# Hybrid encoder block: gate products added into the merged rows by transfers, in the last branch's seven-product scheme

## The chip, the cores and the metric

One core of one Trainium2 chip. The core has a matrix engine (PE; its weight loads are listed apart as PEld), a vector engine (DVE), a scalar engine (ACT), GpSimd (POOL) and SyncE (SP), each with its own in-order queue of instructions, and 16 DMA engines that move the transfers which SP, ACT and POOL issue. The metric is device microseconds of one execution, as the median of several runs.

## The reference

One layer of an encoder, applied to 256 + 512 = 768 tokens of width 1024 in float32. Three token mixers (a state-space branch, a differential attention, a cross-attention) give `branches`, which are projected, gated, merged and projected again:

```python
br = jnp.einsum('blnc,ncd->blnd', branches, w_branch[li])
gates = jax.nn.sigmoid((gl + b_gate[li]).astype(F32)).reshape(Bsz, L, N_BRANCH, D_MODEL)
merged = jnp.sum(gates * br.astype(F32), axis=2).astype(x.dtype)
x = x + merged @ w_out[li]
```

A SwiGLU feed-forward block with its own norm and residual follows. The kernel computes a sigmoid as (1 + tanh(x/2)) / 2 and puts the factor 1/2 where merged is split (below).

## The kernel before, in words

**Precision.** Every float32 operand of a large product is split into a high and a low float32r part, and a product is three matmuls per block of 128 (`mm3`, L755 to L757): high x high, high x low, low x high. The high part is an ACT copy, the low part a DVE subtraction of the high part from the source.

**Stages.** Norm and projections, state-space scan, differential attention, cross-attention; then the branch projections (w_branch2 and w_branch0 as plain products in `branch`, w_branch1 in `branch7`), w_out (`out_rows`), the feed-forward blocks and the down projection. The change is in `branch7` and in the weight stream's `_split_w` for it.

**branch7** (L1648 to L1700) multiplies w_branch1 (1024 x 1024) with the 1024 x 768 output of the differential attention by a seven-product scheme of the Strassen-Winograd kind. It works in four chunks of 256 output columns; in each, seven products of a 128-wide output block with 384 tokens, each product summing four blocks of 128 (twelve matmuls). The left factors are the weight blocks A11, A12, A22 and sums S1 to S4 of them, made per chunk; the right factors B11, B21, B22, T1 to T4 are made once, before (L1616 to L1653; T4 lies in the last two rows of MG). One PSUM bank, `chain`, accumulates A11·B11, then also S2·T2, then also S3·T3, and is copied out after each step by ACT; a second, `p5`, takes S1·T1 and later also S4·B22. Two SBUF accumulators, `cs[0]` = (c11, c12) and `cs[1]` = (c21, c22), collect the four output quarters with ACT copies (L1683, L1685, L1687, L1690) and DVE adds from PSUM (`plus`, L1673). They come from the pool `stg`, two buffers with the tag "brr".

**Gates and merge.** For each chunk two rows of gate logits are loaded from DRAM by POOL's queue into tiles `gs[0]`, `gs[1]` (pool `gtp`, two buffers, tag "glr"; L1657), and ACT takes their tanh in place (L1658). `merge(m)` then multiplies (1 + gate) with the accumulator on DVE, in place in `cs[m]` (L1677), adds the product to row 2c + m of `merged` (L1678: on POOL for m = 0, on DVE for m = 1), and splits that row, times 1/2, into MG's high part (ACT, L1679) and low part (DVE, L1680). MG is the left factor of w_out's product. In chunks 0 to 2 the product S4·B22 and merge(0) come ahead of A22·T4 and merge(1); in chunk 3 the other way round, since the last split overwrites T4's place in MG.

**The weight stream.** `WStream` loads weight blocks (SP's queue, L539, three raw buffers), and `_split_w` makes the seven left factors of a block. For w_branch1 (kind "w2", `inplace`) the sums use two buffers: s1 and s2 take one each, s3 takes s1's, and s4 overwrites s2 (POOL, L574, L575, L581, L583). `_factor` splits each left factor into a half of a pair of tiles, high on ACT (L557) and low on DVE (L558); four such pairs rotate (whi and wlo, `bufs=4`), so eight halves are there for the seven factors of a chunk, and a pair is written again when both of its halves have been used. A name such as wl_A in the profile is that of the pair's first factor: wl_A holds a pair that began with an A block, wl_S one that began with a sum. Other weights go through `_split` (ACT L599; DVE L605, or an accumulating transfer from POOL, L603).

**Order.** The kernel is written with a framework that tracks dependences and puts each engine's instructions in order by itself, from a simulation of their times (the context at L2031 is opened with `schedule_with_timeline_sim=True`); the source order is a priority, not the order of execution, except where an instruction is pinned to it. So PE may work on a product of the next chunk while one of this chunk waits for its factor. The order is fixed when the kernel is built.

**Behind it.** `out_rows` (L1720) multiplies rows 0 to 3 of MG (kh = 0) and then rows 4 to 7 (kh = 1) with w_out for six tiles of tokens, and adds the sum to the input x, loaded by POOL (L1707) into the place of T2 and T3.

Of the kernel before, what the change touches and what calls it, by code (L numbers as in the profile page):

```python
# [8 lines left out]
F32 = mybir.dt.float32  # L9
F32R = mybir.dt.float32r  # L10
I32 = mybir.dt.int32
AF = mybir.ActivationFunctionType
# [491 lines left out]
class WStream:  # L504
# [56 lines left out]
    def _split_w(self, i, h, inplace=False):  # L561
        gt = self.nc.gpsimd.tensor_tensor
        add, sub = ALU.add, ALU.subtract
        view = lambda t: t.rearrange("p (k m c) -> p m k c", k=4, m=2)
        new = lambda k: self.sums.tile([128, 4, 128], F32, name=f"ws{i}{k}", tag="ws")
        if h == 0:
            return
        a1, a2 = view(self.raw.pop(2 * i)), view(self.raw.pop(2 * i + 1))
        A11, A21, A12, A22 = a1[:, 0], a1[:, 1], a2[:, 0], a2[:, 1]
        self._factor(i, "A11", A11)  # L570
        s1, s2 = new(0), new(1)
        if not inplace:
            s3, s4 = new(2), new(3)
        gt(out=s1, in0=A21, in1=A22, op=add)  # L574
        gt(out=s2, in0=s1, in1=A11, op=sub)  # L575
        self._factor(i, "A12", A12)
        self._factor(i, "S2", s2)
        self._factor(i, "S1", s1)
        if inplace:
            s3, s4 = new(2), s2  # L580
        gt(out=s3, in0=A11, in1=A21, op=sub)  # L581
        self._factor(i, "S3", s3)
        gt(out=s4, in0=A12, in1=s2, op=sub)  # L583
        self._factor(i, "S4", s4)
        self._factor(i, "A22", A22)

    def _split(self):
        i, h = divmod(self.n_split, 2)
# [42 lines left out]
def hybrid_block(ctx, tc, A, outs, consts):  # L631
    nc = tc.nc
    v, act, gp, pe = nc.vector, nc.scalar, nc.gpsimd, nc.tensor
    mul, add, sub = ALU.mult, ALU.add, ALU.subtract
# [17 lines left out]
    def uid(s):  # L652
        cnt[0] += 1
        return f"{s}_{cnt[0]}"
# [88 lines left out]
    def split_evac(hi, lo, src, scale=None):  # L743

        if scale is None:
            act.activation(hi, src, AF.Copy)
            v.tensor_tensor(out=lo, in0=src, in1=hi.bitcast(F32), op=sub)
        else:
            act.activation(hi, src, AF.Copy, scale=scale)
            v.scalar_tensor_tensor(out=lo, in0=src, scalar=scale, in1=hi.bitcast(F32), op0=mul, op1=sub)  # L750

    def mm3(ps, wh, wl, xh, xl, start, stop, more=False):

        kw = {"skip_group_check": True} if more else {}
        pe.matmul(ps, wh, xh, start=start, stop=False, **kw)  # L755
        pe.matmul(ps, wh, xl, start=False, stop=False, **kw)  # L756
        pe.matmul(ps, wl, xh, start=False, stop=stop, **kw)  # L757
# [67 lines left out]
    def rows_pair(nm, off=16):  # L825
        t = hp_.tile([128, 16 * TOK + 16], F32R, name=nm, tag="X")
        return tuple(t[:, o : o + 8 * TOK].rearrange("p (k t) -> p k t", k=8) for o in (off, off + 8 * TOK))
# [152 lines left out]
    with tc.tile_pool(name="nrm", bufs=1) as pool, tc.tile_pool(name="nrmg", bufs=1) as pg:  # L980
# [35 lines left out]
        for t in range(4):  # L1016

            tc.keep_in_program_order(v.scalar_tensor_tensor(out=xm[t], in0=xm[t], scalar=1.0, in1=xm[t], op0=mul,
                                                            op1=mul, accum_out=mss[:, t : t + 1]))
# [91 lines left out]
    with ExitStack() as c2:  # L1111
# [4 lines left out]
        for c in range(12):  # L1116
            W.by_dma = True
            w = W.get()
            for m in range(2):
                M = 2 * c + m  # L1120
                for sg, (c0, n) in enumerate(SEGS):
# [3 lines left out]
                    out = act.activation(gt[:, 0:n], ps[:, 0:n], AF.Identity, bias=bg[:, M : M + 1])  # L1125
# [372 lines left out]
    with ExitStack() as c5:  # L1498
# [5 lines left out]
        merged = mgp.tile([128, 8, TOK], F32, name="merged")  # L1504
# [86 lines left out]
        for c in range(4):  # L1591
# [8 lines left out]
            for m in range(2):  # L1600
                M = 2 * c + m
# [43 lines left out]
        MG = rows_pair("mgd", 0)  # L1645
        RB["T4"] = tuple(t[:, 6:8].rearrange("p a (b t) -> p (a b) t", b=2) for t in MG)

        def branch7(n_):  # L1648
            for c in range(4):
                w = W.get()  # L1650
                if c == 0:
                    for k in range(4):
                        split_evac(RB["T4"][0][:, k], RB["T4"][1][:, k], t4[:, k])  # L1653
                gs = []
                for m in range(2):
                    g = gtp.tile([128, TOK], F32, name=uid("glr"), tag="glr")
                    gp.dma_start(g, gl_scr[8 * n_ + 2 * c + m])  # L1657
                    act.activation(g, g, AF.Tanh, scale=0.5)  # L1658
                    gs.append(g)
                cs = [stg.tile([128, TOK], F32, name=uid("bs"), tag="brr") for _ in range(2)]  # L1660
                (c11, c12), (c21, c22) = ((t[:, h1], t[:, h2]) for t in cs)
                chain = env.psb("brc")[:, 0:HT]

                def prod(l, r, ps=None, start=True):
                    if ps is None:
                        ps = psd("br")[:, 0:HT]
                    (wh, wl), (xh, xl) = w[l], RB[r]
                    for k in range(4):
                        mm3(ps, wh[:, k], wl[:, k], xh[:, k], xl[:, k], start and k == 0, k == 3, not start)
                    return ps  # L1670

                def plus(o, ps):
                    v.tensor_tensor(out=o, in0=o, in1=ps, op=add)  # L1673

                def merge(m):
                    M = 2 * c + m
                    v.scalar_tensor_tensor(out=cs[m], in0=gs[m], scalar=1.0, in1=cs[m], op0=add, op1=mul)  # L1677
                    (v if m else gp).tensor_tensor(out=merged[:, M], in0=merged[:, M], in1=cs[m], op=add)  # L1678
                    act.activation(MG[0][:, M], merged[:, M], AF.Copy, scale=0.5)  # L1679
                    v.scalar_tensor_tensor(out=MG[1][:, M], in0=merged[:, M], scalar=0.5,  # L1680
                                           in1=MG[0][:, M].bitcast(F32), op0=mul, op1=sub)

                act.activation(c11, prod("A11", "B11", chain), AF.Copy)  # L1683
                plus(c11, prod("A12", "B21"))
                act.activation(c12, prod("S2", "T2", chain, False), AF.Copy)  # L1685
                p5 = prod("S1", "T1")
                act.activation(c22, p5, AF.Copy)  # L1687
                prod("S3", "T3", chain, False)
                plus(c22, chain)
                act.activation(c21, chain, AF.Copy)  # L1690
                if c < 3:
                    plus(c12, prod("S4", "B22", p5, False))
                    merge(0)
                    plus(c21, prod("A22", "T4"))
                    merge(1)
                else:
                    plus(c21, prod("A22", "T4"))
                    merge(1)
                    plus(c12, prod("S4", "B22", p5, False))
                    merge(0)  # L1700

        branch7(1)
        fctx.close()
        x1t = xp.tile([128, TILES, 1024], F32, name="x1", tag="x1")
# [247 lines left out]
    with ExitStack() as c7:  # L1952
# [12 lines left out]
        for i, (p, g) in enumerate(ITEMS):  # L1965
# [10 lines left out]
            for t in range(3):  # L1976
                c = slice(128 * t, 128 * t + 128)
# [3 lines left out]
            if g == NG - 1:  # L1981
                r, f, op = HOME[p]
# [53 lines left out]
```

## Time and profile before

| | |
|---|---|
| median of 3 runs | 1742.41 us (1741.29 to 1743.65) |
| the profiled execution | 1743.06 us |
| its span, first to last instruction | 1741.3 us |
| mean granted PE clock | 0.999 |
| instructions | 29531 |
| DMA moved | 234.09 MB, mean 134 GB/s |
| branch7, first product to first product of w_out | 1120.74 to 1183.75 us |

How to read it: the profile is one execution on the chip; times are microseconds from the span's start unless marked ns. Matmuls overlap in the pipeline, so a matmul's duration is longer than the step from one start to the next, and a busy PE is judged by the steps. In a row of the order of time stand start, duration, engine, line, operation, output <- inputs and shape; in brackets the engine's idle time just before and what ended it. In the view of waits stand the engine and line that waited, what it waited for, the total in us, how often, and the longest. Times on POOL are rough.

### The profile page before, as it was taken

The numbers are of one execution on the slowest core, as the hardware profiler recorded it, in microseconds if no ns is written. First come the engines' busy times: TensorE is split into PE (matmuls) and PEld (weight loads), VectorE is DVE, ScalarE is ACT, GpSimd is POOL, SyncE is SP. The second block draws the span as 40 slices with busy tenths as digits, with TensorE's granted clock in tenths as the row PEclk, the third lists the DMA queues.
The fourth block names the chain that finished last, engine by engine and source line by source line (L and its number), as shares of the span: only waits on it lengthen the run. The fifth ranks groups of instructions, "written<-read, shape, count | busy, mean of one in ns | idle before, by whom it ended". The sixth has DMA issues, their size and how long they took to land.

```text
span 1741.3 us, 29531 instructions
## 1 busy us (share of the span) xinstructions
PE 1726.6 (99%) x11188; PEld 1608.1 (92%) x11188; DVE 1300.5 (75%) x2405; ACT 908.6 (52%) x1924; POOL 302.5 (17%) x308
## 2 busy tenths in 40 slices
PE   9999999999999999999999999999999999999999
PEld 9999988999999999999989888998889999998887
DVE  7665749699999778887886536685598777776775
ACT  7444543776767346877765434353343333334443
POOL 0000000000000100111000001341036555541130
PEclk9999999999999999999999999999999999999999
DMA  7222636755556454745653435335312323239974
GB/s 268 78 85 91 125 120 135 186 125 143 145 159 159 115 140 103 164 91 156 155 165 117 140 116 157 103 111 174 97 55 91 110 91 109 92 110 295 248 157 97
DMA packets 209213, 234.09 MB, mean 134 GB/s; under 512 B 57832, under 2 KB 173296, under 8 KB 209072
## 3 DMA queue, kind: packets, MB, share of 16 engines
q1 hardware_dynamic: 182160, 167.49, 32.0%
q0 software_dynamic: 17440, 58.34, 15.6%
q10 hardware_dynamic: 9472, 6.39, 1.3%
q8 instruction: 88, 1.44, 0.4%
q14 instruction: 53, 0.43, 0.1%
HBM read 165.78 MB, written 41.22 MB: 119 GB/s over the span
## 4 chain that ended last, share of the span: by engine, by line
PE 95%; DVE 2%; ACT 1%; issue 0%; DMA 0%; POOL 0%; SPq 0%; ACTq 0%; DVEq 0%
PE gl L755 4%; PE gl L756 4%; PE gl L757 4%; PE gate L755 3%; PE gate L756 3%; PE up L756 3%; PE gate L757 3%; PE up L755 3%; PE up L757 3%; PE dn L757 3%; PE dn L755 3%; PE dn L756 3%; PE br L755 3%; PE br L757 3%; PE br L756 3%; PE qk L755 3%
## 5 line engine op out<-in xcount | busy, mean ns | idle before, releaser
L599 ACT ACTIVATE wh<-wr 128x1024 fp32r<-128x1024 f32 x116 | 131.9, 1138 | 52.3 <-PE br L756 13.3
L605 DVE TENSOR_TENSOR wl<-wr,wh 128x1024 fp32r<-128x1024 f32 x74 | 99.2, 1342 | 63.5 <-ACT wh L599 61.7
L755 PE MATMUL gl<-H,wh 128*128 128x256 f32 (+1 forms) x384 | 132.2, 344 | 0.0
L757 PE MATMUL gl<-H,wl 128*128 128x256 f32 (+1 forms) x384 | 129.0, 336 | 0.0
L756 PE MATMUL gl<-H,wh 128*128 128x256 f32 (+1 forms) x384 | 128.7, 335 | 0.0
L603 POOL DMA_DIRECT2D wl<-wr x42 | 36.6, 872 | 483.3 <-ACT wl L602 464.1
L755 PE MATMUL qk<-wh,H 128*128 128x256 f32 x384 | 108.3, 282 | 0.0
L756 PE MATMUL qk<-wl,H 128*128 128x256 f32 x384 | 108.0, 281 | 0.0
L757 PE MATMUL qk<-wh,H 128*128 128x256 f32 x384 | 107.3, 279 | 0.0
L558 DVE TENSOR_TENSOR wl_S<-ws,wh_S 128x512 fp32r<-128x512 f32 x84 | 70.7, 863 | 26.2 <-ACT wh_S L557 26.2
L756 PE MATMUL dn<-wld,dxh 128*128 128x512 f32 x231 | 89.6, 389 | 0.0
L755 PE MATMUL dn<-whd,dxh 128*128 128x512 f32 x231 | 89.5, 389 | 0.0
L757 PE MATMUL dn<-whd,dxl 128*128 128x512 f32 x231 | 88.9, 389 | 0.0
L557 ACT ACTIVATE wh_S<-ws 128x512 fp32r<-128x512 f32 x84 | 49.5, 625 | 73.5 <-PE up L756 36.6
L757 PEld LDWEIGHTS gl<-H,wl 128*128 128x128 f32 x384 | 72.0, 188 | 8.1
L756 PEld LDWEIGHTS gl<-H,wh 128*128 128x128 f32 x384 | 72.2, 188 | 7.2
L755 PEld LDWEIGHTS gl<-H,wh 128*128 128x128 f32 x384 | 72.3, 188 | 6.9
L757 PEld LDWEIGHTS qk<-wh,H 128*128 128x128 f32 x384 | 72.6, 189 | 0.6
L755 PEld LDWEIGHTS qk<-wh,H 128*128 128x128 f32 x384 | 72.4, 188 | 0.6
L756 PEld LDWEIGHTS qk<-wl,H 128*128 128x128 f32 x384 | 72.3, 188 | 0.5
L1296 DVE TENSOR_REDUCE nm<-sc 128x1 f32<-128x512 f32 (+1 forms) x96 | 56.7, 597 | 18.1 <-PE sc L1291 17.2
L1298 ACT ACTIVATE p<-sc,nm 128x512 f32<-128x512 f32 (+1 forms) x96 | 58.8, 615 | 14.4 <-DVE nm L1296 13.9
(535 smaller groups left out, 6076.2 us busy)
## 6 DMA issues: line engine op xcount, KB each, us to landing
wr<-in_w_in_dram SPq DMA_DIRECT2D x48, 512.0 KB, 5.0
wr<-in_w_gate_up_dram SPq DMA_DIRECT2D x44, 512.0 KB, 3.6
wl<-wr POOLq DMA_DIRECT2D x42, 512.0 KB, 5.4
wr<-in_w_branch_dram SPq DMA_DIRECT2D x24, 512.0 KB, 4.5
glr<-gl_scr POOLq DMA_DIRECT2D x24, 384.0 KB, 3.5
hid_scr<-fa SPq DMA_DIRECT2D x11, 768.0 KB, 6.4
wr<-in_w_mem_kv_dram SPq DMA_DIRECT2D x16, 512.0 KB, 4.4
wr<-in_w_in_dram SPq DMA_DIRECT2D x32, 256.0 KB, 3.9
```

The lines of the kernel that those rows point to most:

```text
L557: self.nc.scalar.activation(f(hi), src, AF.Copy)
L558: self.nc.vector.tensor_tensor(out=f(lo), in0=src, in1=f(hi).bitcast(F32), op=ALU.subtract)
L599: self.nc.scalar.activation(hi, r, AF.Copy)
L603: self.nc.gpsimd.dma_start(lo, r.bitcast(F32R), accum_op=ALU.add)
L605: self.sub.tensor_tensor(out=lo, in0=r, in1=hi.bitcast(F32), op=ALU.subtract)
L755: pe.matmul(ps, wh, xh, start=start, stop=False, **kw)
L756: pe.matmul(ps, wh, xl, start=False, stop=False, **kw)
L757: pe.matmul(ps, wl, xh, start=False, stop=stop, **kw)
L1296: v.tensor_reduce(out=nm[:, m : m + 1], in_=ps, axis=AX.X, op=ALU.max, negate=True)
L1298: act.activation(pm[:, 0:n], ps, AF.Exp, bias=nm[:, m : m + 1], accum_out=s1s[:, tt : tt + 1] if m == 0 else s2)
```

## The change

In `branch7`, for chunks 0 to 2, `merge` writes the product of gate and accumulator into the gate's tile and adds it to the row of `merged` by an accumulating transfer that POOL issues; the split of the two rows into MG is emitted in the next chunk, behind the copy of c21. In chunk 3 the add is on DVE for both rows, and the split follows at once. The two accumulator tiles change roles in odd chunks. S1's product is emitted ahead of S2's, with the copy of p5 ahead of the copy of c12, and A22·T4 with merge(1) ahead of S4·B22 with merge(0) in all chunks. In `_split_w` the factor of A22 is made ahead of that of S4 for this kind of block alone; blocks of the feed-forward part keep their order.

```diff
--- before.py
+++ after.py
@@ -581,8 +581,8 @@
         gt(out=s3, in0=A11, in1=A21, op=sub)
         self._factor(i, "S3", s3)
         gt(out=s4, in0=A12, in1=s2, op=sub)
-        self._factor(i, "S4", s4)
-        self._factor(i, "A22", A22)
+        for key, src in (("A22", A22), ("S4", s4)) if inplace else (("S4", s4), ("A22", A22)):
+            self._factor(i, key, src)
 
     def _split(self):
         i, h = divmod(self.n_split, 2)
@@ -1645,6 +1645,11 @@
         MG = rows_pair("mgd", 0)
         RB["T4"] = tuple(t[:, 6:8].rearrange("p a (b t) -> p (a b) t", b=2) for t in MG)
 
+        def merged_parts(M):
+            act.activation(MG[0][:, M], merged[:, M], AF.Copy, scale=0.5)
+            v.scalar_tensor_tensor(out=MG[1][:, M], in0=merged[:, M], scalar=0.5,
+                                   in1=MG[0][:, M].bitcast(F32), op0=mul, op1=sub)
+
         def branch7(n_):
             for c in range(4):
                 w = W.get()
@@ -1658,6 +1663,8 @@
                     act.activation(g, g, AF.Tanh, scale=0.5)
                     gs.append(g)
                 cs = [stg.tile([128, TOK], F32, name=uid("bs"), tag="brr") for _ in range(2)]
+                if c % 2:
+                    cs.reverse()
                 (c11, c12), (c21, c22) = ((t[:, h1], t[:, h2]) for t in cs)
                 chain = env.psb("brc")[:, 0:HT]
 
@@ -1674,30 +1681,28 @@
 
                 def merge(m):
                     M = 2 * c + m
-                    v.scalar_tensor_tensor(out=cs[m], in0=gs[m], scalar=1.0, in1=cs[m], op0=add, op1=mul)
-                    (v if m else gp).tensor_tensor(out=merged[:, M], in0=merged[:, M], in1=cs[m], op=add)
-                    act.activation(MG[0][:, M], merged[:, M], AF.Copy, scale=0.5)
-                    v.scalar_tensor_tensor(out=MG[1][:, M], in0=merged[:, M], scalar=0.5,
-                                           in1=MG[0][:, M].bitcast(F32), op0=mul, op1=sub)
+                    v.scalar_tensor_tensor(out=gs[m], in0=gs[m], scalar=1.0, in1=cs[m], op0=add, op1=mul)
+                    if c < 3:
+                        gp.dma_start(merged[:, M], gs[m], accum_op=add)
+                    else:
+                        v.tensor_tensor(out=merged[:, M], in0=merged[:, M], in1=gs[m], op=add)
+                        merged_parts(M)
 
                 act.activation(c11, prod("A11", "B11", chain), AF.Copy)
                 plus(c11, prod("A12", "B21"))
-                act.activation(c12, prod("S2", "T2", chain, False), AF.Copy)
                 p5 = prod("S1", "T1")
                 act.activation(c22, p5, AF.Copy)
+                act.activation(c12, prod("S2", "T2", chain, False), AF.Copy)
                 prod("S3", "T3", chain, False)
                 plus(c22, chain)
                 act.activation(c21, chain, AF.Copy)
-                if c < 3:
-                    plus(c12, prod("S4", "B22", p5, False))
-                    merge(0)
-                    plus(c21, prod("A22", "T4"))
-                    merge(1)
-                else:
-                    plus(c21, prod("A22", "T4"))
-                    merge(1)
-                    plus(c12, prod("S4", "B22", p5, False))
-                    merge(0)
+                if c:
+                    for m in range(2):
+                        merged_parts(2 * c - 2 + m)
+                plus(c21, prod("A22", "T4"))
+                merge(1)
+                plus(c12, prod("S4", "B22", p5, False))
+                merge(0)
 
         branch7(1)
         fctx.close()
```

## Prediction

> **What bounds the kernel now.** I read the page's totals and chain first, then busy time by stage, then the waits of TensorE (PE), then the order of time around each of them.
>
> ```profile
> span 1741.3 us, 29531 instructions
> ...
> PE 1726.6 (99%) x11188; PEld 1608.1 (92%) x11188; DVE 1300.5 (75%) x2405; ACT 908.6 (52%) x1924; POOL 302.5 (17%) x308
> ...
> PE 95%; DVE 2%; ACT 1%; issue 0%; DMA 0%; POOL 0%; SPq 0%; ACTq 0%; DVEq 0%
> ```
>
> PE is busy for 99% of the span and the chain is 95% PE. No product is added or removed by the change, so all it can gain is the time that PE loses in the stage it touches. That stage, branch7, runs from the first product of branch 1 (1120.74) to the first product with w_out (1183.75). In the windows view the columns after the time are busy us and (count) for PE, weight loads, DVE, ACT, POOL, then granted clock, DMA share, GB/s:
>
> ```profile
> 1120.74:1183.75 63.01, 60.56 (x337) 59.72 (x336) 51.49 (x62) 33.86 (x59) 26.93 (x22) 0.97 0.38 119
> 1163.36:1174.62 11.26, 11.26 (x66) 11.11 (x65) 9.77 (x11) 6.85 (x12) 4.92 (x4) 1.00 0.37 122
> ```
>
> Four chunks of seven products of twelve matmuls are 336, the number of weight loads in the first row. The second row is an undisturbed stretch. In the order of time of PE (start, duration, instruction) its ends are the starts at 1163.36 and 1174.45, 64 steps apart: 11.09 / 64 = 0.1733 us a matmul.
>
> ```profile
> 1156.28 0.34 PE L756 MATMUL brc<-ra,wh_A 128*128 128x384 f32 x1
> 1158.74 0.44 PE L757 MATMUL brc<-ra,wl_A 128*128 128x384 f32 x1 [2.12 <-DVE wl_A L558]
> ...
> 1160.17 0.52 PE L755 MATMUL brc<-ra,wh_A 128*128 128x384 f32 x1
> 1160.49 0.52 PE L756 MATMUL brc<-ra,wh_A 128*128 128x384 f32 x1
> ...
> 1163.36 0.34 PE L756 MATMUL brc<-rc,wh_S 128*128 128x384 f32 x1
> ...
> 1174.45 0.34 PE L757 MATMUL br<-rb,wl_S 128*128 128x384 f32 x1
> 1175.12 0.45 PE L755 MATMUL brc<-rc,wh_A 128*128 128x384 f32 x1 [0.33 <-ACT bs L1683]
> ...
> 1179.25 0.34 PE L757 MATMUL br<-mgd,wl_S 128*128 128x384 f32 x1
> 1179.46 0.44 PE L755 MATMUL brc<-rc,wh_S 128*128 128x384 f32 x1
> ```
>
> So the stage needs 336 x 0.1733 = 58.2 us and takes 63.0: **4.8 us are lost**, 0.28% of the run, and no more is to be had here. A chunk needs 84 x 0.1733 = 14.56 us. The loss has three places. Between the starts at 1156.28 and 1163.36 lie 18 steps (18 x 0.1733 = 3.12) that take 7.08: 3.96 lost. About 2.3 of that is the wait itself and the rest mostly a slow clock, steps of 0.32 us (1160.17 to 1160.49) instead of 0.17. At 1174.45 one step takes 0.67, and with the slow refill behind it 0.65 is lost. The remaining 0.2 is at 1179.46. The waits view names the releasers; the third row is all that it has for PE from 1183.75 to the end:
>
> ```profile
> PE brc L757 <- DVE wl_A L558: 2.1, 1, 2.1
> PE brc L755 <- ACT bs L1683: 0.3, 1, 0.3
> ...
> PE gate L755 <- ACT fhi L746: 0.7, 1, 0.7
> ```
>
> Behind the stage PE hardly waits, so what is won or lost here arrives at the end whole.
>
> **The change part by part: removed adds.** Today merge does a fused multiply on DVE (L1677), an add into merged (L1678: POOL for m = 0, DVE for m = 1), then the two halves of MG. From the view of the lines (min/median/max ns):
>
> ```profile
> L1678 POOL TENSOR_TENSOR merged<-merged,bs x4: 1844/2263/2494, 1137.3 to 1188.2; 128x768 f32<-128x768 f32 x4
> L1678 DVE TENSOR_TENSOR merged<-merged,bs x4: 942/948/959, 1144.7 to 1188.0; 128x768 f32<-128x768 f32 x4
> ...
> L558 DVE TENSOR_TENSOR wl_A<-wr,wh_A x60: 677/693/1866, 1106.7 to 1555.6; 128x512 fp32r<-128x512 f32 x60
> ```
>
> Six adds of chunks 0 to 2 become six transfers and both of chunk 3 go to DVE: DVE does two adds instead of four (-1.9 us), POOL none instead of four (-9 us). DVE was not the bound on average (51.49 of 63.01 us), but it is where the large stall comes from:
>
> ```profile
> 1154.24 2.22 POOL L1678 TENSOR_TENSOR merged<-merged,bs 128x768 f32<-128x768 f32 x1 [2.34 <-DVE bs L1677]
> 1156.42 1.71 POOL L574 TENSOR_TENSOR ws<-wr,wr 128x512 f32<-128x512 f32 x1
> ...
> 1155.15 3.54 DVE L558 TENSOR_TENSOR wl_A<-wr,wh_A 128x512 fp32r<-128x512 f32 x2
> ...
> 1171.97 1.84 POOL L1678 TENSOR_TENSOR merged<-merged,bs 128x768 f32<-128x768 f32 x1 [3.29 <-DVE bs L1677]
> ...
> 1173.85 0.85 ACT L1679 ACTIVATE mgd<-merged 128x768 fp32r<-128x768 f32 x1 [0.36 <-POOL merged L1678]
> 1174.60 0.47 ACT L1683 ACTIVATE bs<-brc 128x384 f32<-128x384 f32 x1
> ```
>
> Two low parts that take 2 x 0.69 = 1.4 us elsewhere take 3.54 while POOL's add and its sum L574 run: 2.2 us too long, ending at 1158.69, just ahead of PE's 1158.74. Without the add they end near 1156.5, and PE, idle from 1156.45, waits about 0.1; the clock then stays up. The bounds: all 3.96 return, or, if L574 moves up beside them (its own median stretch is unknown; at most its 1.71), a stall of that length stays. I take the first: **-3.96 + 0.1**.
>
> The second stall is a chain: POOL's add (to 1173.81), ACT's half of MG, the copy of the next c11, PE at 1175.12. After the change the half of MG of a chunk stands behind the c21 copy of the next, and c11 goes to the tile whose fused multiply came first, so neither is ahead of that copy: **-0.65**. What is late next there is ACT's tanh, below.
>
> **Added transfers.** Their nearest rows are the accumulating transfers of L603 (512 KB, POOL's time to issue, then us to landing), those into dch (accumulating, from DRAM), and the plain gate loads L1657 of the same 384 KB:
>
> ```profile
> L603 POOL DMA_DIRECT2D wl<-wr x42: 850/857/1007, 294.7 to 1252.7; - x42
> ...
> DMA to landing us min/median/max: 4.5/5.4/9.5
> ```
>
> ```profile
> L1657 POOL DMA_DIRECT2D glr<-gl_scr x8: 537/554/557, 1114.8 to 1177.9; - x8
> ...
> DMA to landing us min/median/max: 3.1/3.4/4.2
> ```
>
> ```profile
> dch<-in_w_down_dram POOLq DMA_DIRECT2D x15, 512.0 KB, 9.9
> ```
>
> POOL issues six at 0.86 = 5.1 us, less than the adds it loses. A transfer lands after 3.1 (a plain load at its fastest) to 9.9 us; I take L603's median by size, 5.4 x 384/512 = 4.1. The Trainium skill, DMA: Bandwidth & Descriptors, section Anatomy of one DMA, fits 2.0 us plus bytes over 436 GB/s, an estimate of 2.9 us here; for L603's 512 KB that fit gives 3.2 where the row shows 5.4, so the row decides. By the page the wait below would be 1.2 us shorter.
>
> The price is in the gate's tile. There are two, and the next chunk's gate load now waits until the transfer out of its tile has landed, on POOL's queue in order, with the sums for the next weights (L574 to L583) behind it; POOL is busy 26.93 of 63.01 us, which covers 4.1 us a chunk. Then the load takes 3.4 and the tanh 0.85: 8.4 us from the fused multiply to the next one allowed, against 14.56 - 0.95 = 13.6 in a chunk. The slowest, 9.9 + 4.2 + 0.85 = 15.0, would not fit. But ACT runs in order, and the tanh blocks it while the load is out:
>
> ```profile
> ACT glr L1658 <- DMA glr<-gl_scr: 9.4, 6, 2.3
> ```
>
> ```profile
> 1177.24 0.85 ACT L1658 ACTIVATE glr<-glr 128x768 f32<-128x768 f32 x1 [2.17 <-DMA glr<-gl_scr]
> 1177.99 1.04 ACT L599 ACTIVATE wh<-wr 128x1024 fp32r<-128x1024 f32 x1
> 1178.94 0.47 ACT L1685 ACTIVATE bs<-brc 128x384 f32<-128x384 f32 x1
> ```
>
> Queued behind that tanh was the c12 copy for which PE waited at 1179.46: 9.4 us of such waits cost 0.2. If each of the six later tanh stands where it does now and waits 4.1 longer, 24.6 us more cost 0.5 at that rate; nothing if the planner moves them back; 1.5 if ACT runs out of free time (next part). I take **+0.5**.
>
> **At no cost.** Writing the product to gs and the swap move no data. The new emission order has S1 ahead of S2; PE ran it so already (rb at 1174.45 before rc at 1175.12). A22's factor ahead of S4's puts S4 one ACT and one DVE instruction later (0.69), under a whole product (12 x 0.1733 = 2.1 us). If that cover goes, 0.69 a chunk shows. The halves of MG of chunks 0 to 2, a chunk later, are needed only from w_out. The last ones end sooner, with no POOL add in chunk 3 (2.49 at 1188.2), and PE waited for none of them. Six transfers of 384 KB fit a DMA share of 0.38.
>
> Sum: -3.96 + 0.1 - 0.65 + 0.5 = **-4.0 us**. The profiled execution took 1743.06 with a span of 1741.3, 0.65 above the median of the runs; PE's time is the same in all, so I subtract from the median: 1742.41 - 4.0 = **1738.4**, own range 1737.2 to 1740.0.
>
> **Rivals.** *Slower: the gate's round trip fills ACT.* ACT is busy 33.86 of 63.01, so 46% of a chunk, 6.7 us, is free; tanh waits use 9.4 / 3 = 3.1 of it. From 3.6 us of added wait a chunk ACT is the bound: at 4.1 it costs 0.5 a chunk, 1.5 in three; at 7 us, midway between the rows, 3.4 a chunk and 10.2 in all, so -4.8 + 10.2 = +5.4, 1747.8. For it: the tanh already waits for every load but one, and two rows of accumulating transfers show 9.5 and more. Against: 4.1 is near the threshold, and the planner may queue the tanh later. *The stall moves.* The order on every engine comes from a planner's simulated times; new orders bring new gaps. S3 directly behind S2 waits for a copy, as at 1175.12: 0.5 a chunk, 2.0; L574 beside the low parts, up to 1.7. Net -4.8 + 3.7 = -1.1: 1741.3. For it: POOL keeps four sums a chunk that DVE meets. *It does not do what it says:* the planner leaves the low parts where they collide, 1742.4.
>
> On the price of a new gap: a wait of 2.1 was followed by steps of 0.32, one of 0.33 was not. The Trainium skill, TensorE: Matmul & The Clock Gate, Part 1, lets the clock fall only after an idle window of about 3.4 us; the row shows it after 2.3. By the page the clock's part of any new gap would be nothing; by the row a 2 us gap costs 1.5 more.
>
> **How the numbers follow.** Forecast 0.50, the stall moves 0.25, slower 0.22, nothing happens 0.03. A measurement here cannot tell less than about 0.2% (3.5 us) from no change. Of the forecast's range 1737.2 to 1740.0, most lies under 1738.9: faster 0.40; its rest, the moved stall, nothing, and the mild end of the slower case are same: 0.40; slower 0.20. The range goes from 1737.0 (all 4.8 gone, and some spread of the runs) to 1746.5, halfway into the slower case.
>
> **What would show it.** Right: about 58.5 us from the first product of branch 1 to the first of w_out, clock 1.00, no wait on wl_A, low parts near 0.7. Wrong: PE waits for ACT copies behind tanh waits over 3 us (slower), or one new gap of 1 to 2 us (moved); a transfer landing after 7 us or more; or a changed order behind 1183.75 with waits that before does not have.

## The result, and the profile after

The changed kernel takes 1752.91 us (median of 5 runs, 1751.47 to 1753.90) against 1742.41 for the kernel before (5 runs beside them, 1741.29 to 1743.65). The ratio is 1.0060, with a 95% interval of 1.0048 to 1.0072: **10.5 us slower**, where 4.0 us faster had been forecast.

The page's totals and the last line of its chain, after:

```profile
span 1749.7 us, 29539 instructions
...
PE 1728.1 (99%) x11188; PEld 1608.4 (92%) x11188; DVE 1293.9 (74%) x2403; ACT 908.3 (52%) x1924; POOL 298.5 (17%) x310
...
PE 94%; DMA 2%; DVE 1%; ACT 1%; issue 1%; POOL 1%; SPq 0%; ACTq 0%; POOLq 0%
```

The totals hide it: DVE and POOL have less to do, as meant, and PE is as busy as before. New is a DMA share of 2% in the chain. The windows view of the stage, from the first product of branch 1 to the first with w_out:

```profile
1118.65:1190.49 71.84, 61.43 (x338) 59.64 (x336) 48.84 (x63) 36.07 (x61) 28.48 (x30) 0.95 0.54 140
```

The stage has the same 336 weight loads. It takes 71.84 us where 63.01 stood, so it loses 71.84 - 336 x 0.1733 = 13.6 us instead of 4.8. Behind it the first products with w_out run at a slow clock for a while: the first 24 steps take 7.17 us, 5.48 before. 8.8 + 1.7 = 10.5: the whole difference. (The stage begins 2.1 us earlier than in the execution shown of before; that lies ahead of the change, and the spans of the two executions differ by 8.4 for that reason.) PE's order of time around the lost stretches:

```profile
1148.45 0.45 PE L755 MATMUL brc<-rc,wh_S 128*128 128x384 f32 x1 [0.85 <-ACT bs L1695]
...
1164.15 0.45 PE L755 MATMUL brc<-rc,wh_S 128*128 128x384 f32 x1 [1.26 <-ACT bs L1695]
...
1178.15 0.34 PE L757 MATMUL br<-rb,wl_A 128*128 128x384 f32 x1
1183.86 0.69 PE L755 MATMUL brc<-rc,wh_S 128*128 128x384 f32 x1 [5.37 <-ACT bs L1695]
1184.34 0.52 PE L756 MATMUL brc<-rc,wh_S 128*128 128x384 f32 x1
...
1187.54 0.52 PE L757 MATMUL brc<-rc,wl_S 128*128 128x384 f32 x1
1190.49 0.50 PE L755 MATMUL wo<-wh,mgd 128*128 128x512 f32 x1 [2.42 <-ACT bs L1698]
...
1191.79 0.63 PE L757 MATMUL wo<-wh,mgd 128*128 128x512 f32 x1
1192.21 0.63 PE L755 MATMUL wo<-wh,mgd 128*128 128x512 f32 x1
```

Both stalls of the kernel before, on wl_A and on the c11 copy, are gone. In their place PE waits for copies on ACT: three times for that of c12 (L1695), each time before the S3 product, which needs the same PSUM bank, and once, before w_out, for that of c21 (L1698). (One more, of 0.5 us for c22, stands at 1160.34.) The steps of 0.42 us at 1191.79 are the slow clock: from 1191.50 to 1194.77 the granted clock is 0.52. The view of waits, from somewhat ahead of the stage, names what ACT and POOL waited for meanwhile (us in total, times, longest):

```profile
POOL glr L1662 <- DMA merged<-glr: 18.8, 5, 5.5
ACT glr L1663 <- DMA glr<-gl_scr: 16.5, 7, 4.3
...
ACT mgd L1649 <- DMA merged<-glr: 11.6, 6, 3.8
...
PE brc L755 <- ACT bs L1695: 7.5, 3, 5.4
```

The same view of the kernel before has for the tanhs:

```profile
ACT glr L1658 <- DMA glr<-gl_scr: 13.0, 7, 3.6
```

The first of the seven tanh waits lies ahead of the stage in both kernels; without it they are 12.2 us after and 9.4 before. So the three rows above PE's are new or longer: gate loads that wait on POOL for a transfer out of their tile (18.8 us), tanhs that wait on ACT for these loads (2.8 us more in the stage), and splits that wait on ACT for a transfer into `merged` (11.6; in the stage of before the splits waited 4.0 for the engine adds). How one of them becomes the 5.37 is read from ACT's order of time:

```profile
1174.68 0.85 ACT L1649 ACTIVATE mgd<-merged 128x768 fp32r<-128x768 f32 x1 [3.02 <-DMA merged<-glr]
1175.43 0.47 ACT L1694 ACTIVATE bs<-br 128x384 f32<-128x384 f32 x1
1179.78 0.84 ACT L1663 ACTIVATE glr<-glr 128x768 f32<-128x768 f32 x1 [3.88 <-DMA glr<-gl_scr]
1181.64 0.84 ACT L1649 ACTIVATE mgd<-merged 128x768 fp32r<-128x768 f32 x1 [1.02 <-DMA merged<-glr]
1182.39 1.04 ACT L599 ACTIVATE wh<-wr 128x1024 fp32r<-128x1024 f32 x1
1183.34 0.47 ACT L1695 ACTIVATE bs<-brc 128x384 f32<-128x384 f32 x1
```

The last S2 matmul before the c12 copy starts at 1174.69, so the copy could have run at about 1175.9, right behind that of c22. It stands behind a tanh that waits for its load, a split that waits for a transfer, and a weight part: 7.4 us late. And the chain of waits, back from the first product with w_out (start, us, what):

```profile
1169.65 5.01 DMA merged<-glr
...
1174.94 0.45 POOL glr L1662
...
1175.49 6.13 DMA merged<-glr
...
1181.90 3.34 DMA glr<-gl_scr
...
1185.26 0.04 ACT glr L1663
...
1189.21 0.84 ACT mgd L1649
```

The two transfers of a chunk are not under way together. POOL issues the first at 1169.65; the next on its queue is the load into the tile that this transfer reads, which stands at the head of the queue until it has landed; only then, at 1175.49, POOL issues the second transfer, although its product was done on DVE at 1172.5; and the second load waits for that one. From the first issue to the end of the second tanh at 1186.10 are 16.45 us, more than a chunk of products (14.56). The wait of w_out goes back to the same load: behind that tanh ACT makes a weight part, whose low part on DVE stands ahead of the last chunk's add for row 6; the split of that row waits for this add until 1189.21, and the c21 copy stands behind the split.

### The profile page after: what moved, and what is told of

It reads as the page before. It is cut to its first block, busy times and chain, and to the rows that moved or that the text cites. A ratio compares the mean times of both kernels' runs of the same rounds, so it can differ in the third digit from the quotient of the medians.

```text
span 1749.7 us, 29539 instructions
## 1 busy us (share of the span) xinstructions
PE 1728.1 (99%) x11188; PEld 1608.4 (92%) x11188; DVE 1293.9 (74%) x2403; ACT 908.3 (52%) x1924; POOL 298.5 (17%) x310
## 4 chain that ended last, share of the span: by engine, by line
PE 94%; DMA 2%; DVE 1%; ACT 1%; issue 1%; POOL 1%; SPq 0%; ACTq 0%; POOLq 0%
PE gl L755 4%; PE gl L756 4%; PE gl L757 4%; PE gate L755 3%; PE up L756 3%; PE gate L756 3%; PE up L755 3%; PE gate L757 3%; PE up L757 3%; PE dn L756 3%; PE dn L755 3%; PE dn L757 3%; PE br L755 3%; PE br L756 3%; PE br L757 3%; PE qk L756 3%
## 5 line engine op out<-in xcount | busy, mean ns | idle before, releaser
L603 POOL DMA_DIRECT2D wl<-wr x42 | 36.4, 868 | 492.4 <-ACT wl L602 472.2
L1298 ACT ACTIVATE p<-sc,nm 128x512 f32<-128x512 f32 (+1 forms) x96 | 58.8, 615 | 14.1 <-DVE nm L1296 13.6
```

What stands on the lines that cost most here:

```text
L603: self.nc.gpsimd.dma_start(lo, r.bitcast(F32R), accum_op=ALU.add)
L1298: act.activation(pm[:, 0:n], ps, AF.Exp, bias=nm[:, m : m + 1], accum_out=s1s[:, tt : tt + 1] if m == 0 else s2)
```

## The experiments

Each was timed in alternation with the kernel before, whose medians were 1742.05 (first four), 1742.07 (second four) and 1742.32 us (last four). The theory after reading the trace: the transfers cost through ACT's in-order queue, where tanhs and splits that wait for DMAs stand ahead of copies that PE needs. Rivals: their traffic or the extra instructions; the changed order of products; the held gate tiles.

**1. The transfers taken out** (all else as changed; the adds on POOL and DVE as before, from the gates' tiles):

```diff
-                    if c < 3:
-                        gp.dma_start(merged[:, M], gs[m], accum_op=add)
-                    else:
-                        v.tensor_tensor(out=merged[:, M], in0=merged[:, M], in1=gs[m], op=add)
-                        merged_parts(M)
+                    (v if m else gp).tensor_tensor(out=merged[:, M], in0=merged[:, M], in1=gs[m], op=add)
+                    if c == 3:
+                        merged_parts(M)
```

> The changed kernel with one part undone: the products in the gate tiles are added to merged by engines (POOL for m = 0, DVE for m = 1), as before, and not by transfers; the split into MG a chunk later, the swap of the accumulators, the emission order and the factor order stay. Theory (the gate tile is held until its transfer has landed, its reload blocks POOL and then ACT's tanh, and copies behind it come late for PE): without transfers the loss goes, 1738 to 1743 us, and no wait for a transfer into merged. Rival (the new order of products and factors makes the gaps, whatever the adds are): about 1751 still, with PE waiting for copies of c12.

Measured 1745.29 us, ratio 1.0019 (1.0010 to 1.0028): between the two expectations, in neither. Of the 10.5 us, some 7.3 need the transfers; 3.2 do not. Its waits of PE:

```profile
PE wo L755 <- ACT bs L1696: 3.6, 1, 3.6
PE br L755 <- DVE bs L1680: 1.8, 1, 1.8
```

What is left is a wait of w_out for the c21 copy, as in the changed kernel. There is none on wl_A, although POOL's add is back.

**2. The transfers alone** (the kernel before with the gate's tile as the product's place, the six transfers and the later split; orders, factors and accumulators as before):

```diff
-                    v.scalar_tensor_tensor(out=cs[m], in0=gs[m], scalar=1.0, in1=cs[m], op0=add, op1=mul)
-                    (v if m else gp).tensor_tensor(out=merged[:, M], in0=merged[:, M], in1=cs[m], op=add)
...
+                    v.scalar_tensor_tensor(out=gs[m], in0=gs[m], scalar=1.0, in1=cs[m], op0=add, op1=mul)
+                    if c < 3:
+                        gp.dma_start(merged[:, M], gs[m], accum_op=add)
...
```

> The kernel before with the transfers alone: product into the gate tile, six accumulating transfers, split into MG a chunk later, both adds of the last chunk on DVE; source order of the products, roles of the accumulators and order of the factors as before. Theory (transfers hold the gate tiles): slower than before by 6 to 11 us, 1748 to 1753. Rival (the order is what costs): within 3 us of before, 1740 to 1745.

Measured 1752.69 us, ratio 1.0059 (1.0044 to 1.0074): all of the loss.

```profile
PE brc L755 <- ACT bs L1691: 5.8, 1, 5.8
PE wo L755 <- ACT bs L1696: 2.9, 1, 2.9
PE br L755 <- ACT bs L1693: 2.3, 1, 2.3
```

The same picture with the old source order: three waits for copies on ACT. The changed source order, the factors and the swap are not needed for the loss, and do not lessen it. The order that the planner made of it on PE ends with S3 here too, as in the changed kernel; whether that matters is for run 12.

**3. Both transfers ahead of both loads on POOL's queue:**

```diff
-                        gp.dma_start(merged[:, M], gs[m], accum_op=add)
+                        tc.keep_in_program_order(gp.dma_start(merged[:, M], gs[m], accum_op=add))
...
-                    gp.dma_start(g, gl_scr[8 * n_ + 2 * c + m])
+                    tc.keep_in_program_order(gp.dma_start(g, gl_scr[8 * n_ + 2 * c + m]))
```

(`keep_in_program_order` holds an instruction behind the one emitted before it on its engine.)

> The changed kernel with POOL's issue order pinned to the source: both transfers of a chunk are issued ahead of the next chunk's two gate loads, so that the second transfer no longer waits behind a load that waits for the first to land. Theory with the two round trips in series on POOL as the larger part of the loss: half or more comes back, 1743 to 1748. If one round trip (transfer of 5 to 6 us, load of 3.5 to 5) is enough to make ACT late, it stays at 1750 to 1754.

Measured 1750.38 us, ratio 1.0049 (1.0033 to 1.0066): in the second of the two ranges. POOL's waits for transfers fall from 18.8 to 5.5 us and ACT's for loads from 16.5 to 8.4. But of the 10.5 us only 2.2 come back, for the split still stands in the way:

```profile
1181.23 0.84 ACT L1649 ACTIVATE mgd<-merged 128x768 fp32r<-128x768 f32 x1 [4.54 <-DMA merged<-glr]
1181.98 1.04 ACT L599 ACTIVATE wh<-wr 128x1024 fp32r<-128x1024 f32 x1
1182.92 0.47 ACT L1695 ACTIVATE bs<-brc 128x384 f32<-128x384 f32 x1
```

**4. Four gate tiles** (odd chunks put their gates in the place of t4, so a load waits for a transfer of two chunks ago):

```diff
...
+                g4 = t4p.tile([128, 2, TOK], F32, name=uid("g4"), tag="t4") if c % 2 else None
...
-                    g = gtp.tile([128, TOK], F32, name=uid("glr"), tag="glr")
+                    g = g4[:, m] if c % 2 else gtp.tile([128, TOK], F32, name=uid("glr"), tag="glr")
```

> The changed kernel with two more gate tiles: odd chunks load their gates into the place of t4, which is free after the first chunk, so no gate load waits for the transfer of the chunk just before. The transfers stay. Theory (the wait of the reload is the cause): most of the loss goes, 1737 to 1743, tanh waits under 3 us each. Rival (the traffic of the transfers, or the split of merged that waits for them on ACT, is the cause): 1747 to 1752.

Measured 1749.33 us, ratio 1.0041 (1.0026 to 1.0056): the rival's range. My theory that the reload is the main thing was wrong, or rather half of it. ACT's order of time shows the other half again:

```profile
1180.93 0.84 ACT L1649 ACTIVATE mgd<-merged 128x768 fp32r<-128x768 f32 x1 [4.37 <-DMA merged<-glr]
1181.68 1.04 ACT L599 ACTIVATE wh<-wr 128x1024 fp32r<-128x1024 f32 x1
1182.62 0.47 ACT L1696 ACTIVATE bs<-brc 128x384 f32<-128x384 f32 x1
```

This left two rivals: the splits, or the transfers' mere traffic. Run 5 tells them apart.

**5. Four gate tiles, and ACT's copies ahead of the splits** (run 4's edit, and with it):

```diff
-            act.activation(MG[0][:, M], merged[:, M], AF.Copy, scale=0.5)
+            pin(act.activation(MG[0][:, M], merged[:, M], AF.Copy, scale=0.5))
...
-                act.activation(c11, prod("A11", "B11", chain), AF.Copy)
+                pin(act.activation(c11, prod("A11", "B11", chain), AF.Copy))
...
-                act.activation(c21, chain, AF.Copy)
+                pin(act.activation(c21, chain, AF.Copy))
```

(The c22 and c12 copies likewise; pin is `tc.keep_in_program_order`.)

> The changed kernel with four gate tiles and with ScalarE's copies of a chunk (c11, c22, c12, c21) and the splits of the merged rows held in the order of the program, so that both splits stand behind the c21 copy and no copy stands behind a split that waits for a transfer. Theory (what is left of the loss with four gate tiles, 1749.3, is the splits that wait for transfers ahead of copies on ScalarE; the wait of w_out for the c21 copy is a matter of its own): the gaps of 1.2 to 2 us inside the stage go, the 3.2 us ahead of w_out and some 2 us of slow clock behind it stay: 1744 to 1747. Rival (the transfers cost by their traffic or their own instructions, wherever they stand): no change, 1748 to 1751.

Measured **1742.20 us, ratio 0.9998 (0.9989 to 1.0008): the 10.5 us are gone**, below the expected 1744 to 1747, with all six transfers in place (their median landing is 5.4 and 4.3 us by tile). PE's waits in the stage:

```profile
PE wo L755 <- ACT bs L1701: 2.6, 1, 2.6
PE brc L757 <- DVE wl_S L558: 0.8, 1, 0.8
```

No split waits for a transfer on ACT any more, and no copy stands behind one. The traffic of the transfers is not the cause.

**6. The order alone** (the changed order of products, factors and accumulators; merge by engine adds in the accumulator, split right behind):

```diff
-                    v.scalar_tensor_tensor(out=gs[m], in0=gs[m], scalar=1.0, in1=cs[m], op0=add, op1=mul)
-                    if c < 3:
-                        gp.dma_start(merged[:, M], gs[m], accum_op=add)
...
+                    v.scalar_tensor_tensor(out=cs[m], in0=gs[m], scalar=1.0, in1=cs[m], op0=add, op1=mul)
+                    (v if m else gp).tensor_tensor(out=merged[:, M], in0=merged[:, M], in1=cs[m], op=add)
+                    merged_parts(M)
```

> The changed kernel's order of products, its factor order and the swap of the accumulators, with the merge as before: gate product in the accumulator, both engine adds, the split right behind. No transfer, and no gate tile held. TensorE still ends the stage with the S3 product. Theory (S3 last leaves the c21 copy uncovered ahead of w_out, and the rest of the loss came by transfers): 1743 to 1747, with a wait of w_out on the c21 copy of 2 to 4 us. Rival (the order is harmless without the delayed split, whose place on VectorE and ScalarE makes the copy late): 1740 to 1743.

Measured 1746.09 us, ratio 1.0022 (1.0013 to 1.0032): the theory's time, though not its way, for w_out waits 1.7 us and not 2 to 4. The order costs 4 us with no transfer in the kernel, by a DVE add that is late (2.5 us, with a granted clock of 0.50 for 3 us behind it) and by w_out's wait for c21:

```profile
PE br L755 <- DVE bs L1680: 2.5, 1, 2.5
PE brc L757 <- DVE wl_S L558: 2.1, 1, 2.1
PE wo L755 <- ACT bs L1695: 1.7, 1, 1.7
```

**7. The kernel before without POOL's add** (DVE adds both rows):

```diff
-                    (v if m else gp).tensor_tensor(out=merged[:, M], in0=merged[:, M], in1=cs[m], op=add)
+                    v.tensor_tensor(out=merged[:, M], in0=merged[:, M], in1=cs[m], op=add)
```

> The kernel before with one edit: the add of the merged rows that GpSimd made (m = 0) is made by VectorE. It takes the 1.2 us adds off GpSimd, where the weight parts are made, with nothing else changed. If the first two steps of the prediction are right (the GpSimd add stretches the wait on wl_A, 3.96 us, and feeds the 0.65 us chain): 1737.5 to 1739.5. Rival (VectorE is as late with it, or the wait on wl_A comes from the weight chain itself): 1741 to 1744.

Measured 1740.08 us, ratio 0.9991 (0.9981 to 1.0000): the best of all, some 2 us below the kernel before, which is within what a measurement here can tell from no change. It lies between the two expectations. (The adds that it takes off POOL had taken 1.84 to 2.49 us, not 1.2.) The stage loses 61.22 - 58.23 = 3.0 us, but the wait on wl_A is still there, 2.0 us. On DVE the gate's product ahead of the two low parts now takes 2.05 us (0.95 elsewhere) and the low parts 2.35 (1.4 elsewhere):

```profile
1153.06 2.05 DVE L1677 SCALAR_TENSOR_TENSOR bs<-glr,bs 128x768 f32<-128x768 f32 x1
1155.03 2.35 DVE L558 TENSOR_TENSOR wl_A<-wr,wh_A 128x512 fp32r<-128x512 f32 x2
```

The first runs beside POOL's sum L574, the others beside its sum L575:

```profile
1152.62 1.68 POOL L574 TENSOR_TENSOR ws<-wr,wr 128x512 f32<-128x512 f32 x1 [4.01 <-DVE wl_S L558]
1154.37 1.86 POOL L575 TENSOR_TENSOR ws<-ws,wr 128x512 f32<-128x512 f32 x1
```

**8. Gate tiles held, engine adds** (the kernel before with the product in the gate's tile):

```diff
-                    v.scalar_tensor_tensor(out=cs[m], in0=gs[m], scalar=1.0, in1=cs[m], op0=add, op1=mul)
-                    (v if m else gp).tensor_tensor(out=merged[:, M], in0=merged[:, M], in1=cs[m], op=add)
+                    v.scalar_tensor_tensor(out=gs[m], in0=gs[m], scalar=1.0, in1=cs[m], op0=add, op1=mul)
+                    (v if m else gp).tensor_tensor(out=merged[:, M], in0=merged[:, M], in1=gs[m], op=add)
```

> The kernel before with the gate product written to the gate's tile and added from there, by the engines as before; split right behind, order of products as before in the source. It frees the accumulators and holds the gates' tiles until the add, so that the next gate load waits for an add where it waited for a product. Theory (the held gate tile costs by itself little, since an engine add follows within about 2 us): 1741 to 1744. Rival (holding two gate tiles for both chunks is what costs, and the transfers only lengthen it): 1745 to 1749.

Measured 1747.29 us, ratio 1.0028 (1.0019 to 1.0037): the rival's range. But its largest wait is again that of w_out, so this run doesn't show what the held tile costs by itself:

```profile
PE wo L755 <- ACT bs L1690: 4.0, 1, 4.0
```

It shows something else. In the kernel before and in run 7, TensorE ends the stage with S2, A22, S3, S4. In this kernel, in the changed one and in runs 1 to 6 it ends with S4 and then S3, whichever part of the change they hold; here the source order is that of before, and the planner made the new one by itself. So the c21 copy, which reads S3's result, has no product left to hide it.

**9. Copies ahead of the splits with two gate tiles** (run 5's edit for the splits and the c22, c12 and c21 copies, without the extra tiles; c11 free):

```diff
-            act.activation(MG[0][:, M], merged[:, M], AF.Copy, scale=0.5)
+            pin(act.activation(MG[0][:, M], merged[:, M], AF.Copy, scale=0.5))
...
-                act.activation(c21, chain, AF.Copy)
+                pin(act.activation(c21, chain, AF.Copy))
```

> The changed kernel with its two gate tiles, and on ScalarE the c22, c12 and c21 copies of a chunk and the splits held in the order of the program, so that no copy stands behind a split that waits for a transfer. The tanh of a reloaded gate tile still stands ahead of c12 or c21 copies. Theory (two things hold up ScalarE, the split that waits for a transfer and the tanh whose reload waits for one; here only the first is gone): 1745 to 1749. Rival (the splits alone were the cause, the four tiles did nothing): 1741 to 1743. Rival (the reload alone was the cause): 1751 to 1754.

Measured 1748.66 us, ratio 1.0036 (1.0024 to 1.0048), the theory's range. What is left is the tanh whose load waited for a transfer, with the c21 copy and w_out behind it. ACT in order of time:

```profile
1186.37 0.84 ACT L1665 ACTIVATE glr<-glr 128x768 f32<-128x768 f32 x1 [4.25 <-DMA glr<-gl_scr]
1187.11 0.47 ACT L1700 ACTIVATE bs<-brc 128x384 f32<-128x384 f32 x1
```

and PE:

```profile
1187.64 0.80 PE L755 MATMUL wo<-wh,mgd 128*128 128x512 f32 x1 [6.44 <-ACT bs L1700]
```

**10. Run 5 with S4 last** (in the last chunk A22's product held behind S3's on PE, and S4's behind A22's):

```diff
-        pe.matmul(ps, wh, xh, start=start, stop=False, **kw)
+        keep(pe.matmul(ps, wh, xh, start=start, stop=False, **kw))
...
+                            pin if c == 3 and l in ("A22", "S4") else lambda i: i)
```

> The kernel of four gate tiles and ordered copies, with the S4 product of the last chunk held behind A22 and A22 behind S3 on TensorE, so that the stage ends with S4 as before and 24 products (4 us) follow the S3 product. Theory (the 2.6 us wait of w_out on the c21 copy and about 0.5 us of slow clock are the price of S3 being last): 1738 to 1740. Rival (the wait moves: the c21 copy or a DVE add is late all the same): 1741 to 1743.

Measured 1742.55 us, ratio 1.0000 (0.9991 to 1.0010): the rival's range. The wait of 2.6 us ahead of w_out is gone, and one of 2.5 stands ahead of S3:

```profile
1176.79 0.44 PE L755 MATMUL brc<-rc,wh_S 128*128 128x384 f32 x1 [2.53 <-ACT bs L1699]
```

S3 now follows S2 at once, and needs the c12 copy that reads S2's result out of the same bank. That copy stood behind the c22 copy, which waited for the gate's product of the chunk before on DVE (to 1175.83). S3 last and S3 early each expose one copy.

**11. Run 10 with DVE's adds in place of the transfers:**

```diff
-                    if c < 3:
-                        gp.dma_start(merged[:, M], gs[m], accum_op=add)
-                    else:
-                        v.tensor_tensor(out=merged[:, M], in0=merged[:, M], in1=gs[m], op=add)
+                    v.tensor_tensor(out=merged[:, M], in0=merged[:, M], in1=gs[m], op=add)
+                    if c == 3:
                         merged_parts(M)
```

> The same kernel as the one with S4 last, with VectorE's adds in place of the six transfers (splits still later, four gate tiles, ordered copies). Theory (a transfer that nothing waits for is worth little either way, since the stage is TensorE's): within 1.5 us of the kernel with S4 last. Rival (six adds of 0.95 us come back to VectorE, and copies or weight parts are late): 2 us or more above it.

Measured 1743.66 us, ratio 1.0006 (0.9997 to 1.0016): 1.1 us above run 10, within the theory's 1.5 and within the two intervals. Once nothing waits for them, the transfers are worth about 1 us or nothing.

**12. The changed kernel with S4 last** (run 10's edit alone):

```diff
...
+                            tc.keep_in_program_order if c == 3 and l in ("A22", "S4") else lambda i: i)
```

> The changed kernel with one edit: in the last chunk A22 is held behind S3 and S4 behind A22 on TensorE, so that the stage ends with S4. Two gate tiles, transfers and splits as changed. Theory (the 2.4 us wait ahead of w_out and 1.7 us of slow clock behind it go, the waits for c12 copies behind tanh and splits stay): 1747.5 to 1750. Rival (the last products catch the late copies instead): 1752 to 1755.

Measured 1753.38 us, ratio 1.0060 (1.0045 to 1.0075): no gain; the theory (1747.5 to 1750) was wrong, and the rival's moved wait came. W_out no longer waits; S3 does, 9.35 us, for the c12 copy behind the tanh and the split of before:

```profile
1180.65 0.84 ACT L1663 ACTIVATE glr<-glr 128x768 f32<-128x768 f32 x1 [3.71 <-DMA glr<-gl_scr]
1182.51 0.84 ACT L1649 ACTIVATE mgd<-merged 128x768 fp32r<-128x768 f32 x1 [1.02 <-DMA merged<-glr]
1183.26 1.04 ACT L599 ACTIVATE wh<-wr 128x1024 fp32r<-128x1024 f32 x1
1184.20 0.47 ACT L1696 ACTIVATE bs<-brc 128x384 f32<-128x384 f32 x1
```

So the wait of w_out in the changed kernel is not a price of its own that adds to the others: 5.5 + 2.8 us in two places (from start to start, less a step) became 9.5 in one. To take S3 from the end, where it stands in runs 1 to 6 too, gains nothing by itself.

**What the runs settle.** The loss comes from two DMA waits on ACT's in-order queue, each with copies behind it. Taking away the reload's (run 4) leaves +7.3, taking away the split's (run 9) leaves +6.3, taking away both (run 5) leaves +0.1. The two gains alone, 3.2 and 4.2, add up to 7.4 of 10.5: while one of the two waits is there, it hides part of the other. Run 2 shows that the loss needs nothing else of the change, and run 12 that it stays when S3 is not at the end.

Some of it stays open. The planner sets a new order with every edit, and such orders cost 3.2 (run 1), 4.0 (run 6) and 5.2 us (run 8) in kernels without a transfer, so a gain of 2 to 4 us in a single run may be in part the order's. The pins of run 5 could help a kernel without transfers too; there the pins, the four tiles and S4 last together (run 11) are 1.6 us below run 1, small against 10.5. Run 5 also pinned c11, which run 9 did not, so the split of the 10.5 us between the two waits is approximate.

## Why the prediction was wrong

**The step that failed is "Added transfers", +0.5.** The transfers cost 7.3 us in the changed kernel (run 1 takes them out) and 10.6 when they are added to the kernel before (run 2). The step named the right resource, ACT's queue, and priced it wrongly, in four places:

1. *"A transfer lands after ... 4.1".* They land after 5.0 in the median (384 KB; the row of the view of DMA issues is below), 5.0 and 6.1 in the chain above. Scaling L603's 5.4 by size was wrong: three quarters of the bytes took nine tenths of the time. This alone decided little: in run 5, without the loss, one landed after 6.6, in run 10 one after 7.0.

```profile
merged<-glr POOLq DMA_DIRECT2D x6, 384.0 KB, 5.0
```

2. *"8.4 us ... against ... 13.6 in a chunk".* That is one tile's trip. There are two tiles and one POOL queue in order, and the load at its head kept the second transfer back: 16.45 us for both, more than a chunk. The prediction named the load's wait on POOL and listed the weight sums behind it; it left out the one thing behind it that mattered, the other transfer. Run 3 mended this alone, and got back 2.2 us.
3. *"The half of MG of a chunk stands behind the c21 copy of the next".* In the source, yes; on the engine, no. ACT had a split ahead of the c12 copy in the chunk shown, and waited 11.6 us in all for transfers there. The term for this wait was missing altogether. I had read a source order as an execution order, although the kernel's planner is free in it.
4. *"9.4 us of such waits cost 0.2 ... 24.6 us more cost 0.5 at that rate."* A rate taken where waits are covered doesn't hold where they are not. ACT's tanh waits for loads grew by only 2.8 us in the stage (12.2 - 9.4), the splits' waits for transfers, 11.6, are new, and PE lost 8.8 more. What counts is what stands behind the waiting instruction and when PE needs it: one wait of 3.88 and one of 1.02, with a copy behind both, made 5.37 of PE's.

**Removed adds, -3.96 + 0.1 and -0.65.** Both stalls are absent after, so the forecast of the places came true, but not its reason for the first. Run 7 takes POOL's add away and nothing else: the wait on wl_A stays (2.0 us, before 2.1), since POOL's sum L574 now stretches the gate's product ahead of the low parts by 1.1 us and L575 the low parts by 0.95. Run 1 keeps POOL's add and has no wait on wl_A. The bound that I had set aside ("if L574 moves up beside them ... a stall of that length stays") was right in kind. Of the forecast 4.5 us run 7 shows about 2: the short chain at 1174.45 is gone, and what is lost outside these two waits, most of it slow steps, falls from 2.0 to 0.8 us. That this stall is missing in the changed kernel is a matter of its order; which part of it did that, I did not separate.

**At no cost.** The traffic costs nothing that can be measured (run 5, run 11); that was right. The changed order is not free: 4 us in run 6, with no transfer. Nor is the product's new place: run 8 has only that, and with the order that the planner made for it loses 5.2 us. The prediction looked at S1 ahead of S2 and at the factors, and asked what covers them; it did not ask what covers the c21 copy once S3 is the last product.

**The rivals.** "The gate's round trip fills ACT" is what happened, with the wrong mechanism of price. Its 5.4 us came from a transfer of 7 us and ACT's share of free time; the transfers took 5 to 6, ACT was busy 36.07 of 71.84 us, half idle, and the loss was twice those 5.4. A queue in order doesn't need to be full to be late. The range's upper end lay halfway into this rival, and so below the result. "The stall moves" was right in kind too: S3 waits for the copy of S2's result, now 5.37 instead of the 0.5 I gave it, though with other products between the two.

**The landing time and the clock.** The row on accumulating transfers decided rightly against the fit of the Trainium skill, DMA: Bandwidth & Descriptors, section Anatomy of one DMA: the fit's estimate was 2.9 us, the measured median is 5.0. On the clock the waits here do not agree among themselves. Behind the wait of 2.42 ahead of w_out came, 1.3 us later, steps of 0.42 us instead of 0.23, and behind one of 2.53 in run 6 a first step of 0.48 and then steps of 0.32 (granted clock 0.50); behind that of 2.53 in run 10 the steps are 0.29, then 0.17 (granted clock 1.00). The Trainium skill, TensorE: Matmul & The Clock Gate, Part 1, wants some 3.4 us of idleness first; run 10 agrees with it, the changed kernel and run 6 do not.

## What to carry to other kernels

When an add on an engine becomes a transfer, price the reader that now waits for a landing, and list on each in-order queue what stands behind that reader and behind the load that reuses the source tile; both here were on queues that were half idle. Where a planner sets the order, look which copies each product hides before trusting a source order, and hold the copies that the bottleneck engine needs ahead of anything that waits for a DMA. A rate (so many us of waiting cost so much) holds only as long as the cover does.

## What was not expected of the hardware

- A DVE low part of 0.69 us took 1.77 us beside POOL's two-input sums (the changed kernel at 1157.41, run 1 at 1155.11), about as long as beside POOL's add (1.86, run 1 at 1153.32). In run 7, with no POOL add, two of them took 2.35.
- An accumulating transfer of 384 KB from one SBUF tile to another lands after 5.0 us in the median, and a plain load of the same size from DRAM after 3.5 beside it; POOL takes 0.90 us to issue the one, 0.56 for the other.
- Idle time of PE of the same length was followed by slow steps in some places (2.42 in the changed kernel, 2.53 in run 6) and by none in others (2.53 in run 10, 2.62 in run 5). What decides it, these runs do not show.
